# Hybrid backbone block, state space part: the two directions' decay matrices are added by VectorE, and the gate's z tiles use three buffers

## The chip, the cores and the metric

One core of one Trainium2 chip runs the whole kernel. The metric is the time of one execution on the device in microseconds (us), lower is better. A core has TensorE (PE in the profile), VectorE (DVE), ScalarE (ACT), GpSimd (POOL) and SyncE (SP). SP issues nearly all transfers here, from one queue, in order. Every engine works through its own instructions in a fixed order and waits at an instruction until its inputs and its buffers are ready.

## The reference, cut to what matters

The block normalises 1024 latent and 256 context tokens, projects them, runs three mixers (mLSTM, Mamba-2 state space, RG-LRU), projects the result back and ends with an MLP. The change is in the state space mixer, which for each head computes in chunks

```python
def ssd_scan(A, x, dt, Bm, Cm, state):        # once per direction; the outputs are summed
    def step(h, inp):
        cs = jnp.cumsum(dtc * A, axis=1)
        seg = jnp.exp(jnp.where(tril, cs[:, :, None] - cs[:, None], -jnp.inf))
        w = jnp.einsum("btgn,bsgn->btsg", cc, bc)[..., None] * seg * dtc[:, None]
        y = (jnp.einsum("btsge,bsgep->btgep", w, xc)
             + jnp.exp(cs)[..., None] * jnp.einsum("btgn,bgepn->btgep", cc, h))
        ...
def out(y, extra):                            # z is a projected gate
    y = y + d_skip.reshape(NG_B, HPG_B, 1) * xh
    return rmsnorm(y.reshape(z.shape) * jax.nn.silu(z), g_norm)
```

`seg * dtc` is the decay matrix. Since both directions use the same product of `cc` and `bc`, the kernel adds the two directions' decay matrices first and multiplies once.

## The kernel before, in words

The state space part works on chunks of 128 tokens, 8 of them latent, in `ssd_sweep`. In `ssd_chunk` (L1013 to L1057) a chunk has 8 heads in 2 groups. For each group TensorE builds the logarithm of both directions' decay matrices in PSUM (`expL`, into `psl` and `psx`), ScalarE exponentiates them into two SBUF tiles of 128x512 (L866; the tiles are `r` and `r` or `xp` and `xq`), **GpSimd adds the second to the first (L1020)**, and VectorE multiplies the sum by the product of C and B that TensorE left in `psa` or `psb` (L1023). L1020 runs 16 times in all. Then TensorE multiplies the result with the chunk's x: this is "the chunk's own product" below, eight instructions into `psb` and eight into `psa` that read `r` or `xp` and `XB`. It waits for both L1023. The state update (`pst<-r,r`, L991, L989, L972) and the terms from the carried states (L1029) follow, and VectorE adds the skip term into `KV` (L1055). The rows and columns for `expL` come from `rows_cols` (L855, L857, L859 on VectorE; `rbd` and `rbr` are its tiles).

`ssd_gate` (L1058 to L1067) runs once per chunk, some chunks later. It loads the chunk's z (128x512, from `ZD` in DRAM, L1061), GpSimd multiplies it into `KV` (L1062), ScalarE squares the product into the same z tile (L1063), and four small TensorE instructions with `ones` sum the squares (`pst<-ones,wx`). **The z tile comes from the ring `rzk`, which holds one buffer, `WX[1]` (L766)**: a load waits until the sums of the chunk before are done. `ssd_norm`, after chunks 0 to 3 and again after 4 to 7, takes a tile of the same ring for a diagonal matrix (L1073) that TensorE multiplies with `ones`. `WX[1]` and `WX[0]` also take half the tiles of the output projection's weight (L1170, `wx<-in_w_out`), once the gates are over.

TensorE has other work in this stretch. The projections of z, gr and o (`pd<-xh`, `pd<-xl`, 128x512, through `proj`) stand between the chunks' instructions as filler, and the output projection (`psa`, `psl`, `psb`, `psx`, `pd` from `woh`, `wol`, `w`) follows. The order on every engine is made when the kernel is built: a scheduler takes the instruction of the highest priority that its own model of the chip finds ready, so that both edits move instructions in this stretch. `TA`, 128 x 8 x 128, holds the mLSTM part's exponents; only the mLSTM chunks (`rows_cols(TA, ...)`) read it, and they are over when the state space sweep begins.

Of the kernel before, what the change touches and what calls it, by code (L numbers as in the profile page):

```python
# [7 lines left out]
F32 = mybir.dt.float32  # L8
F32R = mybir.dt.float32r
AF = mybir.ActivationFunctionType  # L10
ALU = mybir.AluOpType
# [27 lines left out]
def body(nc, tc, a, out):  # L39
    V, S, G, T, SY = nc.vector, nc.scalar, nc.gpsimd, nc.tensor, nc.sync  # L40
# [11 lines left out]
    def mm(o, l, r, start=True, stop=True):  # L52
        return T.matmul(o, l, r, start=start, stop=stop)  # L53
# [74 lines left out]
    WX = [wst.tile([P, 512], F32, name=f"wx{i}") for i in range(2)]  # L128
# [337 lines left out]
    TA = gp.tile([P, 8, 128], F32R, name="TA")  # L466
# [296 lines left out]
    xq = ab.tile([P, 1286], F32, name="xq")  # L763
    r2 = Ring(a2, 4, 512, "r2")
    rsp = Sub([WX[0]])
    rzk = Sub([WX[1]])  # L766
    r4 = Ring(ab, 2, 1024, "r4")
    r1 = Ring(ab, 6, 260, "r1")
    r4b = Sub(r4.t + [xp2[:, 0:1024], xq[:, 0:1024]])
# [77 lines left out]
    def rows_cols(TXR, c, nh, IR, nr):  # L847
        px = pT.get([P, P])
        T.transpose(px, TXR[:, c, :].bitcast(F32), ident)
        col = [rcol.get([P, P]) for d in range(2)]  # L850
        row = rrow.get([P, P])
        for d in range(2):
            r = slice(32 * d, 32 * d + 32)
            S.activation(out=col[d][r], in_=px[r], func=AF.Identity, scale=SEL[r, 1:2], bias=SEL[r, 0:1])
        V.tensor_scalar(out=row[0:64], in0=px[0:64], scalar1=SEL[0:64, 0:1], scalar2=SEL[0:64, 1:2], op0=ALU.mult, op1=ALU.add)  # L855
        bd = rbd.get([P, nh, P])
        V.tensor_tensor(out=bd[0:64], in0=row[0:64].unsqueeze(1).broadcast_to([64, nh, P]), in1=IB[0:64, 0:nh].unsqueeze(2).broadcast_to([64, nh, P]), op=ALU.mult)  # L857
        br = rbr.get([P, nr, P])
        V.tensor_tensor(out=br[UP], in0=px[UP].unsqueeze(1).broadcast_to([64, nr, P]), in1=IR[UP, 0:nr].unsqueeze(2).broadcast_to([64, nr, P]), op=ALU.mult)  # L859
        return col, bd, br  # L860

    def expL(d, col, bd, h0, out, ring=pL):
        ps = ring.get([P, 4, P])
        mm(ps, col[d], bd[:, h0:h0 + 4, :], start=True, stop=False)
        mm(ps, identR, MK[d].unsqueeze(1).broadcast_to([P, 4, P]), start=False, stop=True)
        S.activation(out=out, in_=ps, func=AF.Exp)  # L866
# [145 lines left out]
    def ssd_chunk(c, xk, xt, cur, upd=None):  # L1012
        t0 = c * P  # L1013
        col, bd, br = rows_cols(TB_, c, 8, IRB, 4)
        W = [r4b.get([P, 8, P]) for d in range(2)]
        for g in range(2):
            w = [W[d][:, 4 * g:4 * g + 4, :] for d in range(2)]
            for d in range(2):
                expL(d, col, bd, 4 * g, w[d], pL2)
            G.tensor_tensor(out=w[0], in0=w[0], in1=w[1], op=ALU.add)  # L1020
            cb = pAB[g].get([P, P])
            mm(cb, bT[64 * g:64 * g + 64, t0:t0 + P], cT[64 * g:64 * g + 64, t0:t0 + P])
            V.scalar_tensor_tensor(out=w[0], in0=w[0], scalar=0.25, in1=cb.unsqueeze(1).broadcast_to([P, 4, P]), op0=ALU.mult, op1=ALU.mult)  # L1023
        CD = []
        for d in range(2):
            pr = pL2.get([P, 4, P])
            mm(pr, SB_[:, d], br)
            cd = r2.get([P, 4, P])
            V.tensor_tensor(out=cd, in0=pr, in1=cT[:, t0:t0 + P].unsqueeze(1).broadcast_to([P, 4, P]), op=ALU.mult)  # L1029
            CD.append(cd)  # L1030
        yb = KV[:, :, t0:t0 + P]
        py = [pAB[g].get([P, 2, P]) for g in range(2)]

        def batch(jobs):
            first = jobs[0]()
            with tc.issue_after(first.ins):
                for job in jobs[1:]:
                    last = job()
            return last

        def intra(g, jj, q):
            return mm(py[g][64 * q:64 * q + 64, jj, :], xt[:, 4 * g + 2 * jj + q, :], W[0][:, 4 * g + 2 * jj + q, :], start=(jj == 0), stop=False)

        def inter(d, jj, q, g):
            e, gr, st_ = 2 * jj + q, slice(64 * g, 64 * g + 64), cur if d == 0 else SBt[:, c, :]
            return mm(py[g][64 * q:64 * q + 64, jj, :], st_[gr, 64 * e:64 * e + 64], CD[d][gr, e, :], start=False, stop=(jj == 1 and d == 0))

        last = batch([lambda g=g, jj=jj, q=q: intra(g, jj, q) for g in (1, 0) for jj in range(2) for q in range(2)])
        if upd is not None:
            with tc.issue_after(last.ins):  # L1050
                nxt = upd()
        with tc.issue_after(last.ins):
            batch([lambda d=d, jj=jj, q=q, g=g: inter(d, jj, q, g) for d in (1, 0) for jj in range(2) for q in range(2) for g in range(2)])
        for j in range(4):
            V.scalar_tensor_tensor(out=yb[:, j, :], in0=xk[:, j, :], scalar=DSK[:, j:j + 1], in1=py[j // 2][:, j % 2, :], op0=ALU.mult, op1=ALU.add)  # L1055
        return nxt if upd is not None else None
# [23 lines left out]
    def ssd_sweep(fill):  # L1080
        cur = None
        t0, dt = PLAN["ss"]
        for i, c in enumerate(ORD[0]):
            with at(t0 + max(0, i - 2) * dt):
                xk = xk_load(c) if c < 8 else None
                xt = xt_load(c) if c else xt_make(xk)
                upd = None
                if i < 9:
                    bt = bt_load(c) if c else ssd_bt(c)
                    xw, dst = scaled(r2, xt, wB, 0, c), rst.get([P, 256])  # L1090
                    upd = lambda: ssd_update(0, c, bt, xw, cur, dst)
                nxt = ssd_chunk(c, xk, xt, cur, upd) if c < 8 else upd()
            cur = nxt
            if c % 2 == 0 and c < 8:
                fill.pop(0)()
            with at(t0 + max(0, i - 2) * dt + dt):
                if c < 8 and c >= 3:
                    ssd_gate(c - 3)
                if c == 6:
                    ssd_norm(0)  # L1100
        with at(t0 + 8 * dt):
            for c in (5, 6, 7):
                ssd_gate(c)
            ssd_norm(1)
# [617 lines left out]
```

## Time and profile before

| | |
|---|---|
| median of 3 runs | 1293.18 us (1292.07 to 1309.28) |
| the profiled execution | 1304.52 us |
| its span, first to last instruction | 1302.6 us |
| TensorE busy | 1228.7 us, 94% |
| VectorE busy | 980.5 us, 75% |
| ScalarE busy | 564.8 us, 43% |
| GpSimd busy | 288.4 us, 22% |
| mean granted TensorE clock | 0.987 of full speed |

The span is the profiled execution without the 1.9 us around it. Times in the rows are microseconds from the span's start. A busy TensorE is not TensorE at its peak, since its instructions overlap. The state space sweep over the latent chunks lies from about 437 to 545 us, its last gates to 567 us, the output projection begins at 557.5 us, and the MLP follows.

### The profile page before, as it was taken

What the parts mean: (1) busy time and instruction counts of PE and PEld (TensorE: products, weight loads), DVE (VectorE), ACT (ScalarE), POOL (GpSimd) and SP (SyncE); (2) the same over time, 40 slices, a digit from 0 to 9 for tenths busy, and PEclk for the clock granted to TensorE, in tenths of its full rate; (3) what the DMA queues carried; (4) which work ended last, traced back from release to release, by engine and by line L of the source; (5) the groups of instructions that cost most, each with busy time, mean ns of one, the idle gap of its engine ahead of it and who ended that gap; (6) DMA issues with size and microseconds to landing.
All of it is one profiled execution on the core that took longest, in us unless ns stands there. A gap on an engine that the chain in (4) does not pass through costs nothing.

```text
span 1302.6 us, 16521 instructions
## 1 busy us (share of the span) xinstructions
PE 1228.7 (94%) x6066; PEld 962.2 (74%) x6066; DVE 980.5 (75%) x1416; ACT 564.8 (43%) x891; POOL 288.4 (22%) x290
## 2 busy tenths in 40 slices
PE   4888898999999889999999999999999999999997
PEld 1566667778786667677888888777787888888886
DVE  3798977787874675666579766677668988989985
ACT  4546572343433324344375524542457433333432
POOL 2431212212321334204500355354200000000000
PEclk9899999999999999899999999999999999999999
DMA  9444402642426522244323779778569243330112
GB/s 318 149 138 138 129 18 81 187 129 71 131 55 194 150 71 72 82 145 138 129 98 131 266 268 315 256 248 293 210 240 366 88 142 117 125 134 1 54 60 97
DMA packets 122789, 196.48 MB, mean 151 GB/s; under 512 B 11126, under 2 KB 71892, under 8 KB 121172
## 3 DMA queue, kind: packets, MB, share of 16 engines
q1 hardware_dynamic: 118676, 180.74, 41.7%
q10 hardware_dynamic: 4032, 14.68, 3.3%
q8 instruction: 48, 0.79, 0.2%
q14 instruction: 33, 0.27, 0.1%
HBM read 140.76 MB, written 54.63 MB: 150 GB/s over the span
## 4 chain that ended last, share of the span: by engine, by line
PE 39%; DVE 10%; DMA 7%; ACT 4%; issue 3%; POOL 2%; SPq 0%; ACTq 0%; POOLq 0%; DVEq 0%
PE pp L53 18%; PE pd L53 11%; PE psx L53 4%; DVE rw L1339 3%; DMA rw<-in_w_mlp_dram 2%; PE psa L53 2%; PE psl L53 1%; PE psb L53 1%; DVE yb L1311 1%; DMA qxl<-HD 1%; DMA ax<-in_w_mlp_dram 1%; DMA wx<-ZD 1%; PE pst L53 1%; DMA wx<-in_w_out_dram 1%; POOL ax L1485 1%
## 5 line engine op out<-in xcount | busy, mean ns | idle before, releaser
L53 PE MATMUL pd<-xh,wht 128*128 128x512 f32 (+1 forms) x304 | 126.1, 417 | 3.2 <-DVE wx L1111 1.7
L53 PE MATMUL pd<-xh,wlt 128*128 128x512 f32 (+1 forms) x304 | 126.6, 418 | 1.7 <-POOL wlt L352 1.7
L53 PE MATMUL pd<-xl,wht 128*128 128x512 f32 (+1 forms) x304 | 123.0, 409 | 3.9 <-DVE xl L235 2.0
L1485 POOL TENSOR_TENSOR ax<-ax,g2B 128x1024 f32<-128x1024 f32 x32 | 88.4, 2771 | 107.4 <-DMA ax<-in_w_mlp_dram 107.4
L53 PE MATMUL pp<-ob,yb 128*128 128x512 f32 x324 | 97.6, 395 | 0.0
L352 POOL TENSOR_TENSOR wlt<-wraw,wht 128x512 fp32r<-128x512 f32 x40 | 58.8, 1471 | 173.5 <-ACT wht L351 139.5
L1684 POOL TENSOR_TENSOR ss<-ss,V 128x1 f32<-128x1 f32 x8 | 5.1, 643 | 357.0 <-DVE ss L1683 357.0
L1339 DVE TENSOR_TENSOR rw<-rw 128x1024 f32<-128x1024 f32 (+1 forms) x33 | 61.8, 1875 | 28.4 <-DMA rw<-in_w_mlp_dram 28.1
L53 PEld LDWEIGHTS pp<-ob,yb 128*128 128x128 f32 x324 | 60.7, 187 | 14.8
L53 PEld LDWEIGHTS pd<-xh,wht 128*128 128x128 f32 (+1 forms) x304 | 58.1, 191 | 18.1 <-DVE wx L1111 2.2
L53 PEld LDWEIGHTS pd<-xl,wht 128*128 128x128 f32 (+1 forms) x304 | 57.9, 191 | 16.3 <-DVE xl L235 4.9
L53 PEld LDWEIGHTS pd<-xh,wlt 128*128 128x128 f32 (+1 forms) x304 | 58.0, 191 | 14.1 <-POOL wlt L352 2.5
L351 ACT ACTIVATE wht<-wraw 128x512 fp32r<-128x512 f32 (+2 forms) x50 | 28.5, 581 | 62.8 <-PE pd L53 17.3
L53 PE MATMUL pp<-ob,wht 128*128 128x512 f32 x144 | 53.5, 395 | 0.0
L1400 ACT ACTIVATE pp<-pp,V 128x512 f32<-128x512 f32 x35 | 23.0, 657 | 52.3 <-DVE pp L1395 52.1
L1310 ACT ACTIVATE ya<-rw 128x1024 fp32r<-128x1024 f32 x26 | 27.4, 1056 | 40.7 <-issue 14.2
L53 PE MATMUL psx<-xc,wht 128*128 128x256 f32 (+1 forms) x192 | 42.2, 289 | 1.4 <-POOL xc L235 0.7
L53 PE MATMUL pp<-ya,wlt 128*128 128x512 f32 x124 | 43.0, 391 | 0.0
L1311 DVE TENSOR_TENSOR yb<-rw,yb 128x1024 fp32r<-128x1024 f32 x17 | 28.2, 1656 | 14.2 <-ACT yb L1310 14.2
L53 PEld LDWEIGHTS psx<-xc,wht 128*128 128x128 f32 (+1 forms) x192 | 32.9, 183 | 7.9 <-POOL xc L235 1.2
L1311 DVE TENSOR_TENSOR ya<-rw,ya 128x1024 fp32r<-128x1024 f32 x18 | 26.8, 1492 | 15.8 <-ACT ya L1310 15.8
L53 PE MATMUL pp<-yb,wlt 128*128 128x512 f32 x88 | 34.3, 390 | 0.0
(838 smaller groups left out, 3466.7 us busy)
## 6 DMA issues: line engine op xcount, KB each, us to landing
ax<-in_w_mlp_dram SPq DMA_DIRECT2D x33, 512.0 KB, 5.7
rw<-in_w_mlp_dram SPq DMA_DIRECT2D x32, 512.0 KB, 7.0
W2S<-ax SPq DMA_DIRECT2D x32, 512.0 KB, 3.6
wraw<-in_w_in_dram SPq DMA_DIRECT2D x44, 256.0 KB, 2.9
radt<-in_w_ada_dram SPq DMA_DIRECT2D x40, 256.0 KB, 2.9
ada<-in_w_ada_dram SPq DMA_DIRECT2D x16, 512.0 KB, 5.4
HD<-wraw ACTq DMA_DIRECT2D x14, 512.0 KB, 5.6
HD<-g1B ACTq DMA_DIRECT2D x14, 512.0 KB, 3.7
```

The costliest lines, as they stand in the source:

```text
L53: return T.matmul(o, l, r, start=start, stop=stop)
L351: S.activation(out=ph, in_=pr, func=AF.Copy)
L352: (V if split or name[0:2] == "xr" else G).tensor_tensor(out=pl, in0=pr, in1=ph.bitcast(F32), op=ALU.subtract)
L1310: S.activation(out=hi[:, c], in_=src[:, c], func=AF.Copy)
L1311: (e or V).tensor_tensor(out=lo[:, c], in0=src[:, c], in1=hi[:, c].bitcast(F32), op=ALU.subtract)
L1339: RS[2] = (e or V).tensor_tensor(out=q[o], in0=q[x0], in1=q[x1], op=op)
L1400: S.activation(out=ps, in_=ps, func=AF.Relu, bias=V2[:, 40 + f:41 + f])
L1485: G.tensor_tensor(out=u, in0=u, in1=g, op=ALU.mult)
L1684: G.tensor_tensor(out=rs, in0=ss[:, 1:2], in1=MHALF, op=ALU.pow)
```

## The change

The add L1020 moves from GpSimd to VectorE, and `rzk` gets two more buffers, the two halves of `TA`. Nothing else is edited; from the second edit on, line numbers are higher by one.

```diff
@@ -763,7 +763,8 @@
     rsp = Sub([WX[0]])
-    rzk = Sub([WX[1]])
+    TAF = TA.rearrange("p c f -> p (c f)").bitcast(F32)
+    rzk = Sub([WX[1], TAF[:, 0:512], TAF[:, 512:1024]])
     r4 = Ring(ab, 2, 1024, "r4")
@@ -1017,7 +1018,7 @@
             for d in range(2):
                 expL(d, col, bd, 4 * g, w[d], pL2)
-            G.tensor_tensor(out=w[0], in0=w[0], in1=w[1], op=ALU.add)
+            V.tensor_tensor(out=w[0], in0=w[0], in1=w[1], op=ALU.add)
             cb = pAB[g].get([P, P])
```

The scheduler's order moves with it. **First place, VectorE at the first latent chunk** (`r_1711` and `r_1712` are the two directions' tiles, `rbr` and `rbd` the tiles of the next chunk's rows). Before:

```order
L855 TENSOR_SCALAR rrow_1727<-pst_561,SEL 64x128
L859 TENSOR_TENSOR rbr_1722<-pst_561,IRB 64x512
L857 TENSOR_TENSOR rbd_1720<-rrow_1727,IB 64x1024
L1023 SCALAR_TENSOR_TENSOR r_1711<-r_1711,psa_563 128x512
L1023 SCALAR_TENSOR_TENSOR r_1711<-r_1711,psb_564 128x512
L1029 TENSOR_TENSOR r_1707<-psl_565,cT 128x512
L1029 TENSOR_TENSOR r_1708<-psx,cT 128x512
```

With the change:

```order
L856 TENSOR_SCALAR rrow_1727<-pst_561,SEL 64x128
L860 TENSOR_TENSOR rbr_1722<-pst_561,IRB 64x512
L1021 TENSOR_TENSOR r_1711<-r_1711,r_1712 128x512
L858 TENSOR_TENSOR rbd_1720<-rrow_1727,IB 64x1024
L1024 SCALAR_TENSOR_TENSOR r_1711<-r_1711,psa_563 128x512
L1021 TENSOR_TENSOR r_1711<-r_1711,r_1712 128x512
L1030 TENSOR_TENSOR r_1707<-psl_565,cT 128x512
L1024 SCALAR_TENSOR_TENSOR r_1711<-r_1711,psb_564 128x512
L1112 SCALAR_TENSOR_TENSOR wx_93<-wx_93,pd_65 128x512
L1030 TENSOR_TENSOR r_1708<-psx,cT 128x512
```

The two adds (L1021) stand on VectorE itself, one of the two L1030 moves ahead of the second multiplication, and the evacuation of a z projection (L1112) comes in from the next chunk.

**Second place, TensorE ahead of the first latent chunk's own product** (`psb_564<-r_1711,XB`); rows with a plus come in with the change:

```order
 L53 MATMUL pd_65<-xh_87,wht 128x512
 L53 MATMUL pd_65<-xl_88,wht 128x512
+L53 MATMUL pd_65<-xh_87,wlt 128x512
+L850 MATMUL pst_561<-ident,TB 128x128
+L53 MATMUL pd_66<-xh_85,wht 128x512
+L53 MATMUL pd_66<-xl_86,wht 128x512
+L53 MATMUL pd_66<-xh_85,wlt 128x512
+L53 MATMUL pd_66<-xh_85,wht 128x512
+L53 MATMUL psl_565<-rbd_1720,rcol_1725 128x512
+L53 MATMUL psl_565<-MK_591,identR 128x512
+L53 MATMUL pd_66<-xl_86,wht 128x512
 L53 MATMUL psb_564<-r_1711,XB 64x128 x4
```

Nine instructions, eight of them 128x512, now stand ahead of the product; they are taken from later places. At the other seven chunks, too, more instructions stand between the last `expL` results that the chunk needs and its own product (9 or 10 projection instructions instead of 5 or 6 at chunks 3 to 6).

**Third place, SP's queue at the z loads** (`wx_94` is `WX[1]`; XTD, BTD and XSD feed the chunks). Before, from the first z load on:

```order
L1061 DMA wx_94<-ZD 128x4x128
L959 DMA XB<-XTD 128x512
L996 DMA r_1716<-BTD 128x128
L954 DMA XB<-XSD 128x4x128
L338 DMA wraw<-in_w_in_dram 128x4x128
L1112 DMA ZD<-wx_93 128x512
```

With the change:

```order
L1062 DMA wx_94<-ZD 128x4x128
L1062 DMA TA<-ZD 128x4x128 x2
L338 DMA wraw<-in_w_in_dram 128x4x128
L1113 DMA ZD<-wx_93 128x512
L960 DMA XB<-XTD 128x512
L997 DMA r_1716<-BTD 128x128
L955 DMA XB<-XSD 128x4x128
```

Three z loads stand together, and the last spill of z stands ahead of the next chunk's loads instead of behind them. The z loads of chunks 5, 6 and 7 stand together in the same way later.

## Rows read from the trace of the kernel before

**Rows 1.** Windows: stretch, length, busy us (xcount) of PE/PEld/DVE/ACT/POOL, clock, DMA share, GB/s.

```profile
437.00:480.00 43.00, 37.41 (x315) 26.41 (x314) 31.24 (x58) 14.79 (x29) 14.81 (x11) 0.97 0.30 89
460.00:470.00 10.00, 9.12 (x107) 6.41 (x99) 9.68 (x17) 2.99 (x6) 2.58 (x2) 1.00 0.25 64
480.00:545.00 65.00, 61.66 (x442) 45.46 (x440) 40.44 (x81) 23.04 (x43) 28.21 (x22) 1.00 0.23 65
545.00:590.00 45.00, 41.89 (x166) 32.66 (x167) 28.90 (x52) 22.82 (x42) 4.35 (x3) 0.89 0.51 160
545.35:553.00 7.65, 7.65 (x24) 6.30 (x25) 3.63 (x7) 4.36 (x9) 1.19 (x1) 0.55 0.54 174
560.00:567.00 7.00, 5.49 (x22) 4.19 (x20) 3.19 (x11) 4.88 (x9) 2.46 (x2) 0.76 0.29 91
600.00:1300.00 700.00, 687.81 (x3009) 558.60 (x3008) 547.06 (x590) 301.31 (x443) 127.50 (x70) 1.00 0.49 172
```

**Rows 2.** Waits, 437 to 590 us: total us, times, longest.

```profile
POOL KV L1062 <- DMA wx<-ZD: 27.4, 6, 8.3
...
DVE xp L1023 <- POOL xp L1020: 10.8, 7, 4.7
...
DVE r L1023 <- POOL r L1020: 8.7, 5, 4.8
...
PEld psb L53 <- DVE xp L1023: 5.3, 4, 2.8
...
PEld pst L53 <- ACT wx L1063: 4.2, 3, 2.0
PEld psb L53 <- DVE r L1023: 3.9, 4, 2.0
...
PE psb L53 <- DVE xp L1023: 3.6, 2, 2.3
...
PE pst L53 <- ACT wx L1063: 3.1, 2, 1.6
...
PE psb L53 <- DVE r L1023: 2.2, 3, 1.6
...
PE psl L53 <- DVE rbd L857: 1.4, 2, 0.7
...
PE psb L53 <- ACT w L1171: 1.2, 1, 1.2
```

**Rows 3.** Timeline of GpSimd, second and third chunk: start, length, instruction, [idle before].

```profile
453.85 1.28 POOL L1020 TENSOR_TENSOR xp<-xp,xq 128x512 f32<-128x512 f32 x1
455.09 1.19 POOL L1062 TENSOR_TENSOR KV<-KV,wx 128x512 f32<-128x512 f32 x1
456.24 1.26 POOL L1020 TENSOR_TENSOR xp<-xp,xq 128x512 f32<-128x512 f32 x1
463.48 1.29 POOL L1020 TENSOR_TENSOR r<-r,r 128x512 f32<-128x512 f32 x1 [5.98 <-ACT r L866]
```

**Rows 4.** Timeline of VectorE, same stretch.

```profile
457.53 0.69 DVE L1023 SCALAR_TENSOR_TENSOR xp<-xp,psb 128x512 f32<-128x512 f32 x1 [1.68 <-POOL xp L1020]
...
463.53 1.78 DVE L972 TENSOR_TENSOR r<-XB,wB 128x512 f32<-128x512 f32 x1
```

**Rows 5.** Timeline of TensorE's weight loads at the second chunk's own product.

```profile
458.27 0.42 PEld L53 LDWEIGHTS psb<-xp,XB 128*64 128x64 f32 x8 [2.79 <-DVE xp L1023]
```

**Rows 6.** Line 972, 430 to 560 us: count, least/median/most ns.

```profile
L972 DVE TENSOR_TENSOR r<-XB,wB x9: 677/684/1780, 430.1 to 509.5; 128x512 f32<-128x512 f32 x9
```

**Rows 7.** Tile wx, 430 to 600 us, columns as in rows 6.

```profile
L1172 DVE TENSOR_TENSOR wol<-wx,woh x6: 684/693/693, 570.1 to 587.8; 128x512 fp32r<-128x512 f32 x6
```

**Rows 8.** Chain that ended last, 538 to 547 us: start, length, what.

```profile
540.55 2.83 DMA wx<-ZD
...
543.45 1.19 POOL KV L1062
...
545.35 1.51 PE pst L53 x8
```

## Prediction

> **What bounds the kernel now.** I read the table of engines first: TensorE is busy 1228.7 of 1302.6 us, so only time in which TensorE idles, or runs at a low clock, can be won. The windows come second, to see where such time lies near the change and whether time won there lasts to the end. Behind the state space part TensorE is busy 687.81 of 700 us [rows 1]: the MLP has nearly no slack in which an earlier start would be lost, so a microsecond won before 590 us is a microsecond of the total. From 437 to 590 us TensorE's idle time is 43 − 37.41 plus 65 − 61.66 plus 45 − 41.89, which is 12.0 us [rows 1]. The clock adds a loss of its own. In 545.35 to 553 us the mean granted clock is 0.55, so for the most part the lower of its two levels, 1.2 GHz, and in 560 to 567 us it is 0.76 [rows 1]. That is 7.65 × 0.45 plus 7 × 0.24, together 5.1 us of full-speed work. So about 17 us lie in this stretch, and the two edits reach only part of them.
>
> The waits come third. GpSimd waits 27.4 us for z loads, which looks like the largest item, but what TensorE sees of it is 3.1 us in its matmul rows and 4.2 us in its weight-load rows [rows 2]. (A weight load can wait while the matmul before it still runs: the matmul row is the lower, the weight-load row the upper bound of what a wait costs TensorE.) VectorE waits 10.8 + 8.7 = 19.5 us for GpSimd's adds, and TensorE in turn waits for VectorE's multiplications, at the chunks' own products: 5.3 + 3.9 = 9.2 us by the weight loads, 3.6 + 2.2 = 5.8 us by the matmuls [rows 2]. The timelines show how this comes about. At the second chunk GpSimd ends the first add, does the gate's multiplication for 1.19 us, and only at 456.24 begins the second add [rows 3]. VectorE idles 1.68 us for it and multiplies at 457.53 [rows 4], and the product's first weights are loaded at 458.27, after a wait of 2.79 us [rows 5].
>
> **The change, part by part.**
>
> *The adds on VectorE.* On GpSimd an add takes 1.26 to 1.29 us [rows 3]; sixteen are 20.5 us. VectorE's price for it is in no row of L1020; the nearest are L1172, of the same shape and also from two SBUF tiles, 0.693 us [rows 7], and L972, 0.684 us [rows 6]. I take 0.684: VectorE gets 16 × 0.684 = 10.9 us of work and loses 19.5 us of waiting [rows 2]. It was busy 31.24 of the first 43 us and 40.44 of the next 65 [rows 1]; with half of the adds in each that becomes 36.7 and 45.9, or 85% and 71%. So its own idle time covers the work, and it costs nothing on the path except in a crowded stretch (the first rival).
>
> *The wait of the products.* At the second chunk the second add and its multiplication took 458.22 − 456.24 = 1.98 us, after 1.19 us behind the gate [rows 3, 4]; on VectorE the pair takes 0.68 + 0.69 = 1.37 us and stands behind no gate. The new order also puts more filler ahead of the product, nine or ten projection instructions where five or six stood; at 687.81 / 3009 = 0.23 us for one [rows 1], four more are 0.9 us. Of that chunk's 2.79 us [rows 5], 0.61 + 1.19 + 0.9 = 2.7 us go. Taken for all chunks, that is nearly all of the wait, so the bounds are −9.2 above and, if VectorE's own queue gives two thirds of 5.8 back, −2 below. I take −5.5 us, near the 5.8 of the matmul rows, since the second chunk's row says that nearly all of it goes.
>
> *Lesser waits.* TensorE waits 1.4 us for the rows' tile `rbd` [rows 2]; the rows are now made further ahead, and GpSimd's adds no longer shut VectorE out. On the other side the adds lengthen VectorE's way to the chunk's last instruction, L1055. −1 us, between −1.4 and +1 (one add of 0.68 us on the way once, with some waiting).
>
> *The z tiles.* With one buffer a load starts only when the sums of the gate before are done; then the load of 2.83 us, the multiplication of 1.19, and the square follow one another until the sums start at 545.35 [rows 8]. With three buffers the loads stand together and land before their chunk is ready, so that the load leaves this chain. From the multiplication's start to the sums, 545.35 − 543.45 = 1.9 us stay [rows 8], and at the last gate there is little filler to cover them. Of 3.1 to 4.2 us [rows 2] I take −2.5 (0 to −4.2).
>
> *The clock.* Both stretches of low clock begin at such sums, after TensorE had been idle: one at 545.35 [rows 8], the other at the last gate, in 560 to 567 us [rows 1]. Without the wait the fall may go too, but at the last gate a wait remains. Half of 5.1: −2.5 us (0 to −5.1).
>
> *Other queues.* GpSimd loses 20.5 us of work, worth nothing by itself. On SP the z loads stand earlier, and a spill of z has moved ahead of three loads that feed the next chunk, by one issue; I take 0, because nothing in the waits above names those loads. The output projection's weight uses `WX[1]` after the gates; the second norm's diagonal still holds it, and some weight loads that stood ahead of that wait in SP's queue now stand behind it. TensorE waits 1.2 us for a weight now [rows 2]. I take 0 (the second rival prices it).
>
> The sum is −5.5 − 1 − 2.5 − 2.5 = **−11.5 us**. The profiled execution took 1304.52 us, 11.3 us above the median of 1293.18; the sum gives 1293.0 against the one and **1282 us** against the other, and the latter is my forecast, since no term depends on which execution one takes.
>
> One rule speaks against the first edit. The trace has it as one row: L972, with a median of 0.684 us, once took 1.78 us [rows 6], at 463.53, while GpSimd's add ran from 463.48 to 464.77 [rows 3, 4]. VectorE stood until GpSimd was done. The Trainium skill, "SBUF — State Buffer", section "Who interferes with whom", has this as a rule: a VectorE instruction with two SBUF inputs and a GpSimd instruction that reads SBUF exclude each other, and the later of them is fully blocked. By that rule all sixteen moved adds can be blocked by what GpSimd still does. In rows: GpSimd keeps 14.81 + 28.21 − 20.5 = 22.5 us of work in 108 us [rows 1], a fifth, so three or four adds would lose some 0.6 us each, 2 us on VectorE; and each add that left GpSimd blocks nobody. The two about cancel, so the sum has no term for it, and the 2 us stand in the first rival.
>
> **The rivals.**
>
> *1. VectorE sets the pace of the crowded chunks, and the kernel gets slower.* In 460 to 470 us VectorE is already busy 9.68 of 10 us [rows 1]. In a chunk in which it has no idle time every add is a delay: four such chunks have eight adds, 8 × 0.684 = 5.5 us, and 2 us of blocking come on top; if the z part then gives nothing, that is 1293 + 7.5 = 1301 us. It decides from the point at which VectorE has less idle time in a chunk than its two adds take, 1.4 us. Against it: 43 − 31.24 = 11.8 us of idle time in the first four chunks [rows 1], most of it spent in waiting for the adds themselves. Chance 0.12.
>
> *2. The end gives it back.* The sweep gets shorter as forecast, but the second norm and the weight loads behind its diagonal come no earlier, so the output projection waits for its weight longer than the 1.2 us of now [rows 2]. One chain of a load, as long as that of 2.83 us [rows 8], and two conversions of 0.69 [rows 7] is 4.2 us, so 1286 us; with a second such chain 1290. For it: the projection starts earlier by all that is won. Against it: `WX[0]` and three weight tiles behind it work ahead. Chance 0.22.
>
> *3. It is hidden.* The products' waits go over to what is next, the exponentials and the state terms, since the order was made for a model of the chip and not for this trace: 1293 us, 1290 to 1296. Chance 0.1.
>
> *4. All comes back*: 9.2 + 1.4 + 4.2 + 5.1 = 20 us, 1273 us. Chance 0.06.
>
> That the edit doesn't do what it says is no rival: the order shows the adds on VectorE and the three loads side by side.
>
> **How the numbers follow.** The forecast has 0.5; its own range, by its bounds, is 1274 to 1290. The rivals have 0.12, 0.22, 0.1 and 0.06. The range for 8 in 10 goes from 1270, a little under the fourth rival, to 1297, above the third and short of the first; that the runs of before lie between 1292.07 and 1309.28 is a further reason not to end it at 1293. About 2%, 25.9 us, is what a measurement of this kernel can tell from no change: under 1267 or above 1319. The former takes more than all 20 us: 0.03. The latter takes more than three times the first rival: 0.02. Within 2%: 0.95.
>
> **What would show it.** In the changed kernel's waits TensorE's weight loads should wait some 2 to 3 us for the multiplication (now L1024), not 9.2, and GpSimd should have no L1021. The wait for the squares (L1064) should be near 1.5 us, at the last gate alone, and the low clock in the first of its two places should be gone. The first rival would show as windows with VectorE busy over 9.5 of 10 us and TensorE idle beside it; the second as longer waits of TensorE for ScalarE's and VectorE's conversions of the weight (L1172, L1173), with a sweep that ends 10 us sooner while the MLP starts only 5 us sooner. The forecast is wrong if the products still wait over 5 us, or if the time is above 1290.

## The result, and the profile after

The changed kernel takes 1286.45 us (median of 20 runs, 1283.04 to 1292.27), the kernel before 1298.86 us in the same comparison (20 runs, 1291.49 to 1309.28). The ratio is 0.990, 95% interval 0.9885 to 0.9916: 12.4 us faster by the medians, where the forecast said 11.5. The three runs known at the forecast had a median of 1293.18, which is 5.7 us lower than the twenty have; that is why the predicted time, 1282, is 4.4 us too low although the gain is right. The profiled execution of the changed kernel took 1287.25 us, near its median.

The windows of the changed kernel, columns as in [rows 1]:

```profile
437.00:480.00 43.00, 42.57 (x336) 30.64 (x337) 40.19 (x71) 17.90 (x33) 9.90 (x7) 0.96 0.37 108
480.00:545.00 65.00, 62.67 (x453) 47.01 (x452) 49.45 (x88) 26.87 (x50) 14.94 (x11) 1.00 0.23 68
545.00:590.00 45.00, 42.75 (x188) 32.69 (x188) 35.87 (x62) 21.32 (x42) 11.36 (x9) 1.00 0.50 156
447.00:457.00 10.00, 9.88 (x84) 7.04 (x83) 9.94 (x19) 5.64 (x11) 2.88 (x2) 1.00 0.60 169
457.00:467.00 10.00, 9.69 (x81) 6.62 (x81) 9.94 (x19) 3.63 (x7) 1.57 (x1) 1.00 0.19 54
```

Against [rows 1], TensorE's idle time from 437 to 590 us is 0.4 + 2.3 + 2.3 = 5.0 us instead of 12.0, and the clock from 545 to 590 us is 1.00 instead of 0.89. VectorE is busy 40.19 and 49.45 us in the first two windows, 9 us more in each; the adds are 10.9 of these 18 us, the rest is other work that now falls into the two windows. Note the last two rows, ten microseconds each: VectorE is busy 9.94 of 10 us in both, and yet TensorE beside it is busy 9.88 and 9.69.

The waits of TensorE's matmuls, 437 to 590 us (total, times, longest):

```profile
PE psb L53 <- DVE r L1024: 1.2, 1, 1.2
PE psb L53 <- ACT woh L1172: 1.0, 1, 1.0
...
PE psl L53 <- DVE rbd L858: 0.7, 2, 0.3
PE psb L53 <- DVE xp L1024: 0.4, 1, 0.4
PE psa L53 <- DVE KV L1056: 0.3, 1, 0.3
```

The products wait 1.2 + 0.4 = 1.6 us instead of 3.6 + 2.2 [rows 2]. Of the waits for the squares (L1064; 3.1 us in [rows 2]) there is no row any more.

The second chunk on VectorE, and then its product's weight loads on TensorE:

```profile
455.58 0.67 DVE L1021 TENSOR_TENSOR xp<-xp,xq 128x512 f32<-128x512 f32 x1
...
456.78 0.67 DVE L1024 SCALAR_TENSOR_TENSOR xp<-xp,psb 128x512 f32<-128x512 f32 x1
```

```profile
457.85 0.42 PEld L53 LDWEIGHTS psb<-xp,XB 128*64 128x64 f32 x8 [0.37 <-DVE xp L1024]
```

The add (L1021) ends and the multiplication behind it, at 456.78, finds its input there; between them stands a multiplication of another term. The product waits 0.37 us where it waited 2.79 [rows 5].

The sixteen adds on VectorE, eight on each pair of tiles, columns as in [rows 6]:

```profile
L1021 DVE TENSOR_TENSOR r<-r,r x8: 674/682/1003, 443.6 to 526.5; 128x512 f32<-128x512 f32 x8
L1021 DVE TENSOR_TENSOR xp<-xp,xq x8: 673/686/1157, 453.0 to 537.0; 128x512 f32<-128x512 f32 x8
```

The median is 0.68 us, as taken from L972 and L1172 [rows 6, 7]. The longest, 1.00 and 1.16 us, ran while a GpSimd instruction did (L352 from 442.79 us, L1063 from 536.41 us).

The end of the sweep, first on the chain that ended last and then as the tile TA's instructions:

```profile
544.61 0.98 PE pst L53 x8
...
548.69 0.78 PE pst L53 x8
```

```profile
L1063 POOL TENSOR_TENSOR KV<-KV,TA x3: 1202/1557/1641, 508.8 to 545.9; 128x512 f32<-128x512 f32 x3
L1064 ACT ACTIVATE TA<-KV x3: 633/635/636, 510.3 to 547.5; 128x512 f32<-128x512 f32 x3
```

The chain now runs through TensorE's own work, and no z load is in it, where [rows 8] had the load, the multiplication and the wait. GpSimd still takes 1.2 to 1.6 us for a gate and ScalarE 0.64 us, but TensorE has other work meanwhile.

Two profiled executions differ in places the change doesn't touch, so it helps to cut out the stretch. It begins with the z projection at 436.49 us before and at 436.88 after (TensorE waits 1.69 us for VectorE ahead of it in both), and its end is the last transposition ahead of the MLP, at the end of these rows (line 1266, now 1267):

```profile
L1266 PE MATMUL pst<-ident,xn x64: 272/273/327, 596.6 to 672.7; 128*128 128x128 f32 x64
```

```profile
L1267 PE MATMUL pst<-ident,xn x64: 272/273/329, 583.3 to 660.6; 128*128 128x128 f32 x64
```

From 436.49 to 672.7 are 236.2 us, from 436.88 to 660.6 are 223.7 us: 12.5 us, which is the timed difference. What the two profiled executions differ by beyond it, 17.3 − 12.5 us, lies behind it, in the MLP: 1302.6 − 672.7 = 629.9 us against 1285.4 − 660.6 = 624.8.

### The profile page after: what moved, and what is told of

Same layout as the page of the kernel before. It is cut to its first block, busy times and chain, and to the rows that moved or that the text cites. A ratio compares the mean times of both kernels' runs of the same rounds, so it can differ in the third digit from the quotient of the medians.

```text
span 1285.4 us, 16507 instructions
## 1 busy us (share of the span) xinstructions
PE 1224.7 (95%) x6066; PEld 960.5 (75%) x6066; DVE 991.5 (77%) x1432; ACT 565.9 (44%) x891; POOL 270.7 (21%) x274
## 4 chain that ended last, share of the span: by engine, by line
PE 61%; DVE 10%; DMA 6%; ACT 3%; issue 2%; POOL 0%; SPq 0%; ACTq 0%; POOLq 0%; DVEq 0%
PE pp L53 22%; PE pd L53 20%; PE psx L53 7%; PE psa L53 3%; PE psb L53 3%; PE psl L53 2%; DMA wx<-in_w_ada_dram 2%; PE pst L53 2%; DMA rw<-in_w_mlp_dram 1%; DVE wx L727 1%; DVE rw L1340 1%; DMA wx<-in_w_out_dram 1%; DMA qxl<-HD 1%; DMA HD<-g1B 1%; DVE ya L1312 1%
## 5 line engine op out<-in xcount | busy, mean ns | idle before, releaser
L352 POOL TENSOR_TENSOR wlt<-wraw,wht 128x512 fp32r<-128x512 f32 x40 | 59.7, 1493 | 173.7 <-ACT wht L351 143.5
```

The costliest lines, as they stand in the source:

```text
L352: (V if split or name[0:2] == "xr" else G).tensor_tensor(out=pl, in0=pr, in1=ph.bitcast(F32), op=ALU.subtract)
```

## Experiments

Two readings go with every run below: the ratio to the kernel before on the same chip, with its interval, and from its own profile the length of the stretch, TensorE's waits in the matmul rows of 437 to 590 us (at the products for VectorE's multiplication, at the gates' sums for ScalarE's squares) and the clock loss at 545 to 577 us (length times what the mean clock lacks of 1).

| kernel | ratio (95%) | stretch us | products | squares | clock loss |
|---|---|---|---|---|---|
| before | 1 | 236.2 | 5.8 | 3.1 | 5.1 |
| before, again | – | 232.7 | 5.7 | 3.5 | 3.5 |
| the change | 0.990 (0.9885 to 0.9916) | 223.7 | 1.6 | 0 | 0 |
| the change, again | 0.9915 (0.9889 to 0.9941) | 220.8 | 1.7 | 0 | 0 |
| adds alone | 0.9955 (0.9938 to 0.9972) | 227.2 | 0.7 | 2.1 | 1.7 |
| three z buffers alone | 0.9964 (0.9945 to 0.9983) | 229.2 | 7.8 | 0 | 0 |
| two z buffers | 0.992 (0.9898 to 0.9943) | 223.6 | 1.2 | 1.6 | 0 |
| one add of two | 0.9915 (0.9892 to 0.9939) | 226.2 | 4.0 | 0.6 | 0 |
| no add | 0.9884 (0.9858 to 0.9911) | 218.0 | 0 | 0 | 0 |
| extra work, all chunks | 0.9963 (0.994 to 0.9987) | 228.7 | 2.3 | 1.9 | 1.7 |
| extra work, chunks 0 to 3 | 0.9927 (0.9906 to 0.9948) | 226.8 | 1.4 | 1.8 | 1.7 |
| extra work, chunks 4 to 7 | 0.994 (0.9923 to 0.9958) | 228.0 | 3.2 | 0.4 | 1.7 |

Two cautions on reading it. The change has two ratios, 0.990 and 0.9915, which are 2 us apart; distances to the change below are taken from 0.990, and from the other the slower runs are 2 us nearer to it. And a stretch is one execution: those of before, the change, two z buffers, extra work in all chunks and in chunks 0 to 3 also hold some 1.6 us of low clock right at their beginning (0.83 to 0.85 over 437 to 447 us), the others none.

**Each edit alone.** The adds alone:

```diff
-    rzk = Sub([WX[1], TAF[:, 0:512], TAF[:, 512:1024]])
+    rzk = Sub([WX[1]])
```

> Only the adds go to VectorE; z keeps one buffer. My theory: the two edits are worth separate amounts, so this gives the part of the products: TensorE waits there 1 to 2 us instead of 5.8, the rows' tile 0.7 instead of 1.4, and the time is 4 to 6 us below before (ratio 0.995 to 0.997). The waits for the squares stay, 2 to 4 us, and so does a stretch of low clock behind them. Rival: the low clock and the waits for squares come from the whole sweep being late, and the adds alone heal them; then the time is 10 to 13 us below before and the clock stays at 1.00.

Measured: 0.9955, 5.8 us. The products' wait is gone (0.7 us), and sums still wait twice, as TensorE's timeline shows, with the windows behind them:

```profile
543.67 1.05 PE L53 MATMUL pst<-ones,wx 128*128 128x1 f32 x8 [1.08 <-ACT wx L1064]
...
556.26 1.05 PE L53 MATMUL pst<-ones,wx 128*128 128x1 f32 x8 [1.04 <-ACT wx L1064]
```

```profile
547.00:557.00 10.00, 8.96 (x47) 7.20 (x45) 4.50 (x7) 3.77 (x7) 2.39 (x2) 1.00 0.66 207
557.00:567.00 10.00, 9.82 (x35) 7.34 (x36) 7.91 (x17) 6.87 (x14) 1.40 (x1) 0.83 0.40 124
```

The first of the two waits, 1.08 us, has no low clock behind it; behind the second the clock is 0.83. Each edit acts on its own wait here, as my theory had it.

The three buffers alone:

```diff
-            V.tensor_tensor(out=w[0], in0=w[0], in1=w[1], op=ALU.add)
+            G.tensor_tensor(out=w[0], in0=w[0], in1=w[1], op=ALU.add)
```

> Only the z tiles get three buffers; the adds stay on GpSimd. My theory: the waits for the squares (3.1 us) and the clock behind them (5.1 us) go, so 7 to 9 us below before (ratio 0.993 to 0.995), with the products still waiting 5 to 6 us and the clock at 1.00 from 545 to 570 us. Rival: GpSimd's adds still stand ahead of the gate's multiplication in its queue, so that the sums stay late; then 0 to 4 us below before and a stretch of low clock remains.

Measured: 0.9964, 4.7 us, less than the 7 to 9 expected; of what was expected the interval reaches only the edge. The mechanism is as expected: the clock in 545 to 590 us is 1.00, and no wait for squares is left. But other waits grew, which the matmul rows show:

```profile
PE psb L53 <- DVE xp L1024: 4.2, 3, 2.3
PE psb L53 <- DVE r L1024: 3.6, 3, 1.4
PE psl L53 <- DVE rbd L858: 1.7, 3, 0.7
...
PE pst L53 <- DVE wx L1074: 0.7, 1, 0.7
```

The products wait 4.2 + 3.6 = 7.8 us instead of 5.8, and the second norm's diagonal (L1074) and `rbd` cost 0.7 + 1.7 us where they cost 1.4 [rows 2]. By this, 3.1 + 5.1 − 2.0 − 1.0 = 5.2 us should be won, and against the second profile of the kernel before (3.5 + 3.5 − 2.1 − 1.0) 3.9 us; the 4.7 lie between. In this trace part of what the z wait gave went into the products' wait, so the second edit may be worth more with the first than alone. The two alone make 10.5 us and both 12.4, but the intervals are some 2 us each way, so the timed runs do not show this.

**How much room VectorE has.** No add at all (the second direction's matrix is computed and left out of the sum):

```diff
-            V.tensor_tensor(out=w[0], in0=w[0], in1=w[1], op=ALU.add)
```

> The changed kernel without the adds: the second direction's decay matrix is computed but not used. It prices what is left of the adds on VectorE. My theory: they are hidden, so 0 to 2 us below the change, 12 to 15 below before (ratio 0.9885 to 0.991). Rival: the adds on VectorE still delay the products or the chunk's end, and 5 us or more are to be had: 17 us or more below before (ratio under 0.987).

Measured: 0.9884, 2 us below the change, inside its interval. So the sixteen adds, 10.9 us of VectorE's time, cost about 2 us by the times, with an interval of some 4 us either way, and by the stretches 223.7 − 1.6 − 218.0 or 220.8 − 218.0, 4 or 3 us (1.6 us is the low clock at the beginning, which this run doesn't have). They seem mostly but not wholly hidden. The run prices a little more than the adds: without them no VectorE instruction waits for the second direction's exponential either. One more instruction of their size ahead of each:

```diff
+            V.tensor_tensor(out=w[1], in0=w[1], in1=w[1], op=ALU.max)
             V.tensor_tensor(out=w[0], in0=w[0], in1=w[1], op=ALU.add)
```

> The changed kernel with one more VectorE instruction of the same shape ahead of each add (the maximum of the second tile with itself, in place, which changes no value): 16 x 0.684 = 10.9 us more on VectorE, right in the way of the products. My theory: VectorE has idle time and TensorE has filler, so it costs 0 to 4 us against the change, 9 to 13 below before (ratio 0.990 to 0.993). Rival: VectorE is the pace of the crowded chunks already, and each extra instruction there is paid: 7 to 11 us against the change, 2 to 5 below before (ratio 0.996 to 0.999).

Measured: 0.9963, some 8 us above the change. My theory fell: the first 10.9 us on VectorE cost 2 to 4, the next 10.9 some 8 (the interval is clear of the change's). But the timeline of TensorE's matmuls shows that most of the loss is not in the crowded chunks:

```profile
450.66 0.66 PE L53 MATMUL psb<-r,XB 128*64 128x128 f32 x8 [0.80 <-DVE r L1025]
...
467.04 0.49 PE L53 MATMUL psa<-cT,bT 64*128 64x128 f32 x2 [1.10 <-DVE KV L1057]
...
551.54 0.50 PE L53 MATMUL psa<-woh,yh 128*128 128x512 f32 x1 [1.29 <-DVE KV L1057]
...
555.62 1.05 PE L53 MATMUL pst<-ones,TA 128*128 128x1 f32 x8 [1.95 <-ACT TA L1065]
```

```profile
557.00:567.00 10.00, 9.63 (x34) 7.10 (x33) 7.11 (x15) 1.83 (x3) 1.39 (x1) 0.84 0.23 67
```

Waits of 0.80 and 1.10 us stand in the crowded chunks, waits of 1.29 and 1.95 us behind the last chunk, and low clock follows the latter. The instruction order gives one reason. The model by which it is made sees the product come later and puts 14 to 22 projection instructions ahead of it in the first four chunks, where the change has 8 to 12. Projections are a fixed stock, and in this run none is left behind the last product; in the change thirteen follow. That made a new theory, that cover is used up, and two runs to tell it from VectorE's pace:

```diff
+            if c < 4:          # the other run: c >= 4
+                V.tensor_tensor(out=w[1], in0=w[1], in1=w[1], op=ALU.max)
             V.tensor_tensor(out=w[0], in0=w[0], in1=w[1], op=ALU.add)
```

> The second VectorE instruction ahead of each add in chunks 0 to 3 alone, the crowded ones (half of e4's extra work, 5.5 us). Theory after e4: what e4 lost (8 us against the change) was mostly lost behind the last chunks, because the order had used up its filler by then; here filler is left at the end, so only the crowded part is paid, 1 to 3 us against the change, 10 to 12 below before (ratio 0.991 to 0.9925). Rival: VectorE is the pace of the crowded chunks, and nearly all of e4's loss is made there: 5 to 8 us against the change, 5 to 8 below before (ratio 0.994 to 0.996).

> The same in chunks 4 to 7 alone, where VectorE has idle time but where the order leaves no projection behind the last chunk's product. Theory after e4: the larger part of e4's loss, 4 to 7 us against the change, 6 to 9 below before (ratio 0.993 to 0.9955), with TensorE idle and a stretch of low clock at 545 to 570 us. Rival (VectorE's pace): 0 to 2 us against the change, 11 to 13 below before (ratio 0.990 to 0.9915).

Measured: 0.9927 in the first four chunks, some 3.5 us above the change, and 0.994 in the last four, some 5 us above it; together they make the 8 of the run with both. By the times this is the new theory's side, but it is not proven by them: the first run lost a little more than expected, its interval overlaps the change's, and the two runs' intervals overlap. By the stretches the losses are 226.8 − 223.7 = 3.1 and 228.0 − 220.8 = 7.2 us, each against the profile with the same clock at its beginning. The traces are less simple than the theory. In the run with the last four chunks TensorE waits at the very last product, when all projections are done, and VectorE's timeline shows for what:

```profile
546.77 1.12 PE L53 MATMUL psb<-xp,XB 128*64 128x128 f32 x8 [2.48 <-DVE xp L1026]
```

```profile
544.23 0.69 DVE L1132 SCALAR_TENSOR_TENSOR qT<-wx,qT 128x512 f32<-128x512 f32 x1 [1.61 <-ACT wx L1131]
544.84 0.69 DVE L1023 TENSOR_TENSOR xp<-xp,xq 128x512 f32<-128x512 f32 x1
```

The second add, at 544.84, is not late by its own length. It stands behind L1132, the evacuation of the last projection, which waits 1.61 us for ScalarE. An engine that works in order hands on a wait of one piece of work to the next. Later in this run TensorE also waits 2.2 us ahead of the transpositions (L1269), where the change waits 1.0.

In the run with the first four chunks 23 projection instructions are left behind the last product, and still there is a wait for sums at the end. So the stock alone doesn't explain it. A gate's multiplication on GpSimd took 2.83 us there, in place of 1.2:

```profile
546.48 2.83 POOL L1065 TENSOR_TENSOR KV<-KV,TA 128x512 f32<-128x512 f32 x1 [9.41 <-DVE PR L1070]
```

It did so in the run with all chunks too, of which these are GpSimd's row and VectorE's in the same time:

```profile
552.08 2.83 POOL L1064 TENSOR_TENSOR KV<-KV,TA 128x512 f32<-128x512 f32 x1 [10.84 <-DVE PR L1069]
```

```profile
551.99 0.68 DVE L1174 TENSOR_TENSOR wol<-wraw,woh 128x512 fp32r<-128x512 f32 x1
552.59 0.68 DVE L1174 TENSOR_TENSOR wol<-wx,woh 128x512 fp32r<-128x512 f32 x1
553.19 0.68 DVE L1174 TENSOR_TENSOR wol<-wraw,woh 128x512 fp32r<-128x512 f32 x1
```

VectorE runs the weight's splits from 551.99 to 553.87, each with two SBUF inputs and one straight after the other, and GpSimd, which started 0.09 us later, ends 1.04 us after them. By these rows it was shut out until VectorE let go, and behind it stand the squares and TensorE's 1.95 us. In the run with the first four chunks:

```profile
467.73 0.48 PE L53 MATMUL psa<-cT,bT 64*128 64x128 f32 x2 [1.09 <-DVE KV L1058]
...
550.02 1.05 PE L53 MATMUL pst<-ones,TA 128*128 128x1 f32 x8 [1.78 <-ACT TA L1066]
```

```profile
467.00:477.00 10.00, 9.27 (x46) 6.79 (x46) 8.61 (x16) 3.03 (x6) 2.85 (x2) 0.83 0.21 52
547.00:557.00 10.00, 8.22 (x32) 6.13 (x31) 5.45 (x14) 2.51 (x5) 3.69 (x2) 0.83 0.15 53
```

Both waits have low clock behind them, 0.83 over ten microseconds, which is 1.7 us each; the wait of 1.10 us at the same place in the run with all chunks had none.

What the traces show: VectorE's last microseconds of idle time are used by the change, and with more work there TensorE waits, in the crowded chunks (1.09 us at 467 us) and at the end. The times show it for the extra work in all chunks; for chunks 0 to 3 alone they don't resolve it. That the used-up stock alone makes the loss is refuted; how much of the 8 us is due to it stays open.

**Between the two kernels.** Two z buffers:

```diff
-    rzk = Sub([WX[1], TAF[:, 0:512], TAF[:, 512:1024]])
+    rzk = Sub([WX[1], TAF[:, 0:512]])
```

> The change with two z buffers instead of three. Theory: one load ahead is enough, since a load takes 3 us and the sums of two gates are 4 us apart at the closest: as the change, 12 to 14 below before (ratio 0.989 to 0.991). Rival: at the end the third buffer is what counts, because the load of the last gate waits for the sums of the last but two while filler is short: TensorE waits 1 to 2 us there, with low clock behind it, 8 to 11 below before (ratio 0.9915 to 0.994).

Measured: 0.992, in the rival's range, but the interval reaches both, and the change's own second ratio is 0.9915. The trace has the rival's waits, without its low clock: sums wait twice where the change has no such wait, and the clock in 545 to 590 us is 1.00.

```profile
540.56 1.05 PE L53 MATMUL pst<-ones,wx 128*128 128x1 f32 x8 [0.33 <-ACT wx L1064]
...
548.69 1.05 PE L53 MATMUL pst<-ones,TA 128*128 128x1 f32 x8 [1.29 <-ACT TA L1064]
```

At the later of the two GpSimd sat idle for 6.97 us until the load of the last gate but one landed:

```profile
546.80 1.17 POOL L1063 TENSOR_TENSOR KV<-KV,TA 128x512 f32<-128x512 f32 x1 [6.97 <-DMA TA<-ZD]
```

So the third buffer takes away two waits, 0.33 + 1.29 us by these rows. That they lengthen the kernel is not shown: the stretch is 223.6 us against the change's 223.7, and the times don't resolve so little.

One add of each chunk on GpSimd again:

```diff
-            V.tensor_tensor(out=w[0], in0=w[0], in1=w[1], op=ALU.add)
+            (V if g else G).tensor_tensor(out=w[0], in0=w[0], in1=w[1], op=ALU.add)
```

> The change, but the first group's add of each chunk goes back to GpSimd and only the second group's is VectorE's. Theory: the first add is early and needs no haste, and VectorE is relieved of 5.5 us, so the same or a little better than the change: 12 to 16 below before (ratio 0.988 to 0.991). Rival: GpSimd's add stands behind the gate's multiplication or L352 in its queue and shuts VectorE out, so that the products wait again: 7 to 11 below before (ratio 0.9915 to 0.9945).

Measured: 0.9915, at the edge of the rival's range, and by the times not to be told from the change. The trace speaks for the rival: the products wait 4.0 us instead of 1.6, and the stretch is 226.2 us against 220.8 (both without low clock at the beginning). So relieving VectorE by 5.5 us gains nothing:

```profile
PE psb L53 <- DVE r L1024: 2.4, 2, 1.8
...
PE psb L53 <- DVE xp L1024: 1.6, 1, 1.6
```

This run also bears on a rival that the forecast left inside one term: that the products gain from the filler which the new order puts ahead of them, and not from the place of the add. At the sixth chunk nine projections stand right ahead of the product here and ten in the change. First this run, its wait on VectorE and on TensorE, then the change:

```profile
520.50 0.69 DVE L1024 SCALAR_TENSOR_TENSOR xp<-xp,psa 128x512 f32<-128x512 f32 x1 [1.19 <-POOL xp L1021]
...
523.03 0.66 PE L53 MATMUL psb<-xp,XB 128*64 128x128 f32 x8 [1.60 <-DVE xp L1024]
```

```profile
513.31 0.66 PE L53 MATMUL psb<-xp,XB 128*64 128x128 f32 x8 [0.44 <-DVE xp L1024]
```

The one projection is, at the forecast's 0.23 us, the smaller part of the difference of 1.16 us; the other 0.9 us go with VectorE's wait for GpSimd's add. So the filler alone does not take the wait away. How the 4 us of all products divide between the two is not shown, since no run has the old order with the new adds.

**Both kernels again.** For the clock, which the forecast took half of.

> The kernel before once more, for a second profile: is the low clock behind the late sums (5.1 us in the first profile) there in every execution? Theory: the sums wait again (2.5 to 3.5 us of TensorE's matmul rows) and the products too (5 to 7 us), and at least one stretch of low clock lies at 545 to 570 us, for 1.5 to 5 us. Rival: the low clock comes and goes by itself; then it may stand anywhere, or nowhere, with the same waits.

> The changed kernel once more, beside the experiments' chips. Theory: as in the first profile no wait for sums above 0.5 us, the products 1 to 2.5 us, and no low clock at 480 to 590 us; time 12 to 14 us below before (ratio 0.989 to 0.991). Rival: low clock stands in 480 to 590 us although nothing waits for the sums; then the clock term of the forecast was luck of one profile, and the time is nearer 9 to 11 below (ratio 0.9915 to 0.993).

Measured: the kernel before waits for sums twice again, and low clock lies behind the second wait alone, 2.2 + 1.3 = 3.5 us instead of 5.1:

```profile
548.89 1.05 PE L53 MATMUL pst<-ones,wx 128*128 128x1 f32 x8 [1.60 <-ACT wx L1063]
...
562.56 1.78 PE L53 MATMUL pst<-ones,wx 128*128 128x1 f32 x8 [1.90 <-ACT wx L1063]
```

```profile
547.00:557.00 10.00, 8.40 (x55) 6.94 (x48) 7.10 (x13) 7.41 (x15) 2.72 (x2) 1.00 0.49 156
557.00:567.00 10.00, 8.10 (x31) 6.48 (x30) 5.47 (x15) 5.46 (x11) 3.61 (x2) 0.78 0.40 119
567.00:577.00 10.00, 10.00 (x38) 7.47 (x37) 8.90 (x16) 4.62 (x8) 0.00 (x0) 0.87 0.40 119
```

The changed kernel has a clock of 1.00 in all of 437 to 590 us and no wait for sums, so the rival's low clock is not there. Its ratio is 0.9915, a little above the 0.989 to 0.991 expected, with an interval of 0.9889 to 0.9941, which holds the 0.990 of the first comparison. Stretch against stretch, the second pair of profiles gives 232.7 − 220.8 = 11.9 us, the first 12.5.

The timed executions say more of the clock than two profiles can. Each lists its span and its mean clock, and the span times what the clock lacks of 1 is the loss over the whole execution. In this last comparison it is 16.0 us on average for the kernel before (16 executions, mean clock 0.9877) and 11.8 us with the change (12 executions, 0.9908): 4.2 us, give or take some 2.6. For the three z buffers alone it falls from 17.0 to 15.6 us, 1.4 us give or take some 2, where the profiles fell from 5.1 or 3.5 to 0. So with both edits the clock term holds over many executions; with the buffers alone it is not clear of nothing, and the size of 5.1 us belongs to one profile.

No run beats the change beyond the intervals.

## Why the prediction was right

Term by term, forecast against the two profiles:

| term | forecast us | first profiles | again |
|---|---|---|---|
| the products' wait | −5.5 | 5.8 to 1.6: −4.2 | 5.7 to 1.7: −4.0 |
| the rows' tile and L1055 | −1 | 1.4 to 1.0: −0.4 | 1.4 to 0.3: −1.1 |
| the z tiles | −2.5 | 3.1 to 0: −3.1 | 3.5 to 0: −3.5 |
| the clock | −2.5 | 5.1 to 0: −5.1 | 3.5 to 0: −3.5 |
| the weight's wait | 0 | 1.2 to 1.2: 0 | 0.8 to 0.4: −0.4 |
| sum | −11.5 | −12.8 (stretch −12.5) | −12.5 (stretch −11.9) |

- **What bounds it** was right: time won before 590 us reached the end. The stretch's 12.5 and 11.9 us are the 12.4 us of the medians.
- **The products** were the largest term and oversized: 4 us, not 5.5. At the second chunk, from which the term was taken, the weight loads' wait fell from 2.79 to 0.37 us, near the 2.7 forecast; but a wait of 1.2 us remains at another chunk, and all weight loads together wait 3.6 us for L1024, not 2 to 3. The bounds of the forecast's terms (−9.2 − 1.4 − 4.2 − 5.1 and −2 + 1) make 1273 to 1292 us, not quite the 1274 to 1290 that it states.
- **The z tiles and the clock** were undersized by these profiles. I kept 1.9 us at the last gate as a wait, because multiplication and square still stand ahead of the sums. The rows show them still there, 1.6 + 0.64 us, but projections now stand between and cover them. With the wait the low clock went, in both profiles whole and not by half; over the timed executions the clock gave 4.2 us, with an interval that holds the 2.5. That the sum came out so near is in part luck: the errors of the terms cancel.
- **VectorE's cover**: the adds cost 2 to 4 us by the run without them, against 0 in the forecast. The gain of the edit is what is left after it.
- **The rule** on VectorE and GpSimd shutting each other out: of the sixteen adds three were lengthened, by 0.21, 0.32 and 0.48 us over the median, 1.0 us in all, where I had worked out 0.6 us for each of three or four. What I had not weighed is the other direction: GpSimd's 2.83 us above, at a gate's multiplication that TensorE waits for. The Trainium skill, "SBUF — State Buffer", section "Who interferes with whom", has both directions: the instruction that starts second is the one that is blocked. The trace agrees, since GpSimd started 0.09 us behind VectorE's.
- **Rival 1** (VectorE's pace) did not come, but the point that I gave for it was wrong. VectorE did fall below 1.4 us of idle time in a chunk: 9.94 of 10 us are busy in two windows, and TensorE had other work. With as much again on VectorE the loss came, most of it at the end of the sweep.
- **Rival 2** (the end gives it back) did not come: the weight's wait stayed at 1.2 us, and at 0.4 in the second profile. That its 1286 us is the measured time is chance: the median that it was counted from was 5.7 us too low.

## What to carry to other kernels

Read waits by what the bounding engine loses, not by who waits longest: GpSimd's 27.4 us for z loads were 3.1 us of TensorE's, and in two profiles the clock behind them cost as much again or more. Work that moves to an engine with idle time is cheap only until that idle time is gone; look at windows of one chunk's length, and at the end of the loop, where little other work is left. Compare a stretch between two landmarks of each profile rather than two whole executions.

## What was not expected of the hardware

In this stretch every fall of the clock came with a wait of TensorE of 1 us or more, but most such waits had none behind them, and their length doesn't tell which. At the beginning, behind the same wait of 1.69 us, the clock fell in five of the twelve executions (0.83 to 0.85 over 437 to 447 us) and stayed at 1.00 in the others. At the end of the sweep and in the output projection behind it, waits of 1.04, 1.51, 1.57, 1.78, 1.90, 1.95 and 2.48 us had low clock with them, and waits of 1.04, 1.08, 1.25, 1.29 (twice) and 1.60 us had none. In the middle the longest wait, 2.35 us ahead of the second chunk's product in the kernel before and about the same in its second profile and with three z buffers alone, had a clock of 1.00 behind it each time. So a wait costs its length and, in some executions, another 1.7 to 3.5 us of clock; why some are spared stays open.
